# Gates and convolved inputs of layers 2 to 4 as z (1 + tanh(z/2)) in a four-layer hybrid decoder

## Chip, cores and metric

The kernel runs on one core of one Trainium2 chip. The metric is the device time of one execution in microseconds (us), the median over several runs. The core has a matrix engine (PE, with its weight loads shown as PEld), a vector engine (DVE), a scalar engine (ACT), GpSimd (POOL), and queues that move data between HBM and the on-chip memory SBUF; matmul results land in PSUM, from where ACT or DVE take them.

## What is computed

256 tokens of width 1024 pass four layers, each with another mixer (S5, gated linear attention, differential attention, Mamba-2 SSD), and each layer also attends to 256 memory tokens. Layers are counted 1 to 4 in the title and 0 to 3 in the code; below they have the code's numbers.

```python
for i in range(DEPTH):
    h = rms_norm(x, norm_g[i])
    # h @ W_in -> mixer inputs | z_mix | z_x | q_mem
    # every mixer ends in a gate by silu(z); layers 1 to 3 also normalise:
    #   gla:  rms_norm(o, norm_g) * silu(z)
    #   diff: rms_norm(o, subln_g) * (1 - lam_init) * silu(z)
    #   ssd:  xbc = silu(causal_depthwise_conv(xbc)); ... ; rms_norm(y * silu(z), norm_g)
    mem_out = memory_cross_attention(qx, mem_n, w_mem_kv[i], xq_g[i], xk_g[i]) * jax.nn.silu(z_x)
    x = x + jnp.concatenate([branch, mem_out], axis=-1) @ w_out[i]
```

silu(z) is z sigmoid(z), which equals z (1 + tanh(z/2)) / 2.

## The kernel before

All weights are streamed. SP's queue brings a raw tile of 128x1024 (L211); ACT rounds it to the matmul's number format (`hi`, L114, a cast), DVE takes the rest (`lo = raw - hi`, L115), and each product is made of three matmuls (`mm3`, L227 to L229: hi by hi, lo by hi, hi by lo). The right side is `hT`, the normalised activations, split in the same way, or `hT` is the weight side and the tile moves.

Projections are generators in a list, `fill`. A mixer's own code calls `tick` at chosen points, which lets the generator at the list's head issue a few more matmuls, so that PE has projection work between the mixer's small matmuls. Which instruction stands where on each engine's queue is settled by a scheduler ahead of time from the program, its priorities (scores are issued at a raised priority) and its estimates of durations; on the chip every engine then takes its own queue strictly in order and waits at an instruction whose inputs or buffers aren't ready.

PSUM is held in three small buffers (`ps`), one more (`ps2`) and two accumulators (`acc`) of two banks each. A matmul that starts a new accumulation waits until the reader of the old one is done.

The places that the change touches:

- `qx_zx_steps` (L456): the gate z_x of the memory attention, Silu by ACT from PSUM.
- Layer 1: `evac_z` (L940), the gate of a head, 128x1024, Silu by ACT from `acc`.
- Layer 2: `evac_z` (L1181), the same. `attend` computes scores (L1199) whose maximum DVE takes (L1200, L1202), exponentials on ACT (L1204), the difference of the two softmaxes on DVE (L1208 to L1210, tile `pr`), its transpose on PE (L1220), a copy on ACT (L1222, `wT`) and the product with v on PE (L1224). After the fourth head of a block comes the norm of the block: a copy and a square on ACT (L1231, L1232), sums on DVE (L1234 to L1236), the mean (L105), a power on POOL (L107, tile `rr`), one product (L1238), and four products with the gate (L1241), which PE then transposes (L188).
- Layer 3: `conv` (L1351 on ACT, three steps L1354 on DVE, Silu L1356 on ACT) for the tiles `bm`, `cm` and `xf`, and `evac_z` (L1369). `scan` makes decays: PE fills `ps` (L1400, L1401), ACT takes exponentials from it (L1404, L1405, tile `mt`), DVE multiplies them by dt and by `cb` (L1406, L1407), and PE uses `mt` in L1417. `cb` is a product of `cm` and `bm` that ACT copies out of PSUM (L1392).

Where a function of another kind than the last one runs on ACT, the program holds an instruction ACT_TABLE_LOAD ahead of it, under the line of that function.

Of the kernel before, what the change touches and what calls it, by code (L numbers as in the profile page):

```python
# [12 lines left out]
AF = mybir.ActivationFunctionType  # L13
# [24 lines left out]
class Net:  # L38
# [97 lines left out]
    def all_gains(self):  # L136
        a = self.a
        flat = lambda v: v.rearrange("a b -> (a b)")
        self.mem_g, self.s5_d, self.gla_b, self.ssd_g, self.gla_g, self.diff_g, xq, xk = self.gains("gains", [
            (a["mem_norm_g"], 8), (a["s5_d"][0], 16), (a["gla_b_gk2"][0], 4), (a["ssd_norm_g"][0], 16),  # L140
            (a["gla_norm_g"][0], 4), (a["diff_subln_g"][0], 1), (flat(a["xq_g"]), 4), (flat(a["xk_g"]), 4)], self.nc.sync)
        self.qsc = self.const.tile([P, 4], F32, name="qsc")
        self.nc.vector.scalar_tensor_tensor(self.qsc, xq, float(P) ** -0.5, xk, MUL, MUL)

# [226 lines left out]
    def xattn(self, i, qx, zx, perm=False):  # L371


        nc = self.nc
        kT, v = self.kv
        self.headnorm(qx)
        self.tick()
        qT = self.head_T(qx, self.t4(self.xp, "xt", 3).rearrange("p (h t) -> p h t", h=4), self.qsc[:, i:i + 1])
        zv = zx.rearrange("p (h q) -> p h q", h=4)

        def scores(t):
            rs = self.sm(4, "xrs")
            pr = (self.t4(self.xp, "xt", 3) if t else self.t4(self.xp, "pr")).rearrange("p (h m) -> p h m", h=4)
            sums = self.sm(4, "xsum")
            for hp in range(2):
                s = self.ps().rearrange("p (h m) -> p h m", h=2)
                for hh in range(2):
                    h = hp * 2 + hh
                    nc.tensor.matmul(s[:, hh, :], qT[:, h, t * P:(t + 1) * P], kT[:, h, :], start=True, stop=True)  # L389
                mx = self.sm(2, "xmx")  # L390
                nc.vector.tensor_reduce(mx, s, AX.X, ALU.max, negate=True)
                for hh in range(2):
                    h = hp * 2 + hh
                    nc.scalar.activation(pr[:, h, :], s[:, hh, :], AF.Exp, bias=mx[:, hh:hh + 1],
                                         accum_out=sums[:, h:h + 1])
            nc.vector.reciprocal(rs, sums)
            nc.vector.tensor_tensor(pr, pr, bc(rs, 2, 256), MUL)
            return pr

        self.tick()  # L400
        prs = [scores(0)]
        self.tick()
        prs.append(scores(1))
        pTs = [self.t4(self.xp, "pT"), self.t4(self.xp, "xt", 3)]
        mo = self.t4(self.xp, "xt", 3).rearrange("p (h q) -> p h q", h=4)
        hi = self.t4(self.bp, "xq", 2, F32R).rearrange("p (k t) -> p k t", k=4)
        for hp in range(2):
            pT = pTs[hp].rearrange("p (h m q) -> p h m q", h=2, m=2)
            for hh in range(2):
                tp = self.ps().rearrange("p (m q) -> p m q", m=2)  # L410
                for t in range(2):
                    for mh in range(2):
                        nc.tensor.transpose(tp[:, mh, t * P:(t + 1) * P], prs[t][:, hp * 2 + hh, mh * P:(mh + 1) * P],
                                            self.ident)
                (nc.scalar.copy if hh else nc.vector.tensor_copy)(pT[:, hh], tp)  # L415
            self.tick()
            pv = (self.ps2() if hp else self.ps()).rearrange("p (h q) -> p h q", h=2)
            for hh in range(2):
                h = hp * 2 + hh
                for mh in range(2):  # L420
                    nc.tensor.matmul(pv[:, hh, :], v[:, mh, h * P:(h + 1) * P], pT[:, hh, mh, :], start=mh == 0,  # L421
                                     stop=mh == 1)
            hs = slice(2 * hp, 2 * hp + 2)
            if hp == 0:
                lo = self.t4(self.xp, "pT", 1, F32R).rearrange("p (k t) -> p k t", k=4)
            nc.vector.tensor_tensor(mo[:, hs], pv, zv[:, hs], MUL)
            if perm:
                self.split(mo[:, hs].rearrange("p k (h s j) -> p (k h) s j", h=2, s=4),
                           *(u[:, hs].rearrange("p k (h j s) -> p (k h) s j", h=2, s=4) for u in (hi, lo)))
            else:  # L430
                self.split(mo[:, hs], hi[:, hs], lo[:, hs])
        self.tick()
        return [(hi[:, k, :], lo[:, k, :]) for k in range(4)]

    def silu_tanh(self, z, t):

        nc = self.nc
        nc.scalar.activation(t, z, AF.Tanh, scale=0.5)
        nc.vector.scalar_tensor_tensor(z, t, 1.0, z, ADD, MUL)

    def qx_zx(self, *args):
        out = []
# [4 lines left out]
    def qx_zx_steps(self, out, xT, w, col, silu=True):  # L447

        nc = self.nc

        def evac_z(nb, ps):
            if nb == 0:
                out.append(self.t4(self.bp, "xq", 2))
            z = out[1].rearrange("p (h t) -> p h t", h=4)[:, 2 * nb:2 * nb + 2, :]
            if silu:
                nc.scalar.activation(z, ps, AF.Silu)  # L456
            else:
                nc.scalar.copy(z, ps)

        def evac_q(_, acc, c):  # L460
            out.append(self.t4(self.bp, "xq", 2))
            nc.scalar.copy(out[-1].rearrange("p (t c) -> p t c", t=2), acc)  # L462

        return chain(self.linear_steps(xT, w, col + DX, DX, evac_q),
                     self.linear2_steps(xT, w, col, DX, evac_z, lambda: self.acc()[:, 0, :]))
# [279 lines left out]
    def layer0(self):  # L745
        nc, tc, a = self.nc, self.tc, self.a
        w = a["s5_w_in"][0]
        with self.pool("l0") as lp_:
# [52 lines left out]
            with self.pool("l0b") as p:  # L801
# [47 lines left out]

                self.norm_mem()  # L850
                self.mem_kv(0)
                self.silu_tanh(zx, self.t4(self.xp, "xt", 3))
                nc.vector.tensor_scalar(zx, zx, 0.5, None, MUL)
                self.fill = [self.linear2_steps(gp, a["s5_w_glu"][0], 0, DI, evac_glu)]
                moT = self.xattn(0, qx, zx, True)
                self.drain()
# [23 lines left out]
    def layer1(self):  # L880
# [4 lines left out]
        with self.pool("gla") as p:  # L885
# [51 lines left out]

            def evac_z(_, acc, c):
                vz.append(t4("z", 2))
                nc.scalar.activation(v2(vz[-1]), acc, AF.Silu)  # L940

            def proj(h):
                return chain(self.linear_steps(hT, w, 1024 + h * 512, 512, evac_v),
# [155 lines left out]
    def layer2(self):  # L1099
# [5 lines left out]
        with self.pool("diff") as p:  # L1105
# [11 lines left out]
            V.tensor_scalar(le[:, 3:4], le[:, 2:3], -lam_init, None, ADD)  # L1117
            nlam = le[:, 3:4]
            sg = p.tile([P, 4], F32, name="sg")
            V.tensor_scalar(sg, self.diff_g.to_broadcast([P, 4]), 1.0 - lam_init, None, MUL)  # L1120

            mask = p.tile([P, 256], F32, name="cmask")
            nc.gpsimd.memset(mask, 0.0)
# [49 lines left out]
            def proj(nb, out):  # L1173
                def evac_v(_, acc, c):
                    later.pop()()
                    out.append(t4("v", 2))
                    nc.scalar.copy(v2(out[-1]), acc)

                def evac_z(_, acc, c):
                    out.append(t4("z", 2))  # L1180
                    nc.scalar.activation(v2(out[-1]), acc, AF.Silu)  # L1181

                return chain(qk(nb, 0, *rt[0], out), qk(nb, 2048, *rt[1], out),
                             self.linear_steps(hT, w, 4096 + nb * 512, 512, evac_v),
                             self.linear_steps(hT, w, 6144 + nb * 512, 512, evac_z))
# [92 lines left out]
    def layer3(self):  # L1278
# [5 lines left out]
        with self.pool("ssd") as p:  # L1284
# [59 lines left out]
            def conv(col0, tag, bufs, out):  # L1344


                def evac(_, ps):
                    o = T([P, 2, 256], tag, bufs)
                    for c in range(2):
                        b = col0 // P + c  # L1350
                        nc.scalar.activation(o[:, c, :], ps[:, c, :], AF.Identity, bias=cw[:, 4, b:b + 1],  # L1351
                                             scale=cw[:, 3, b:b + 1])
                        for j in range(1, 4):
                            V.scalar_tensor_tensor(o[:, c, j:], ps[:, c, :256 - j], cw[:, 3 - j, b:b + 1], o[:, c, j:],  # L1354
                                                   MUL, ADD)
                    nc.scalar.activation(o, o, AF.Silu)  # L1356
                    out.append(o)

                return self.linear2_steps(hT, w, col0, 256, evac)
# [5 lines left out]
            def proj(gp, out):  # L1365
                def evac_z(nb, ps):
                    if nb == 0:
                        out.append(T([P, 4, 256], "z", 2))
                    nc.scalar.activation(out[-1][:, 2 * nb:2 * nb + 2, :], ps, AF.Silu)  # L1369

                return chain(conv(2048 + gp * 256, "bm", 2, out), conv(3072 + gp * 256, "cm", 2, out),
                             *(conv((2 * gp + i) * 256, "xf", 4, out) for i in range(2)),
# [2 lines left out]
            def scan(gp, bm, cm, xf0, xf1, zz):  # L1375
# [9 lines left out]
                def decays(b):  # L1385
                    gi, blk = b // 2, gp * 4 + b
                    if b % 2 == 0:
# [1 line left out]
                        nc.tensor.matmul(ps[:, 0:256], bm[:, gi, 0:P], cm[:, gi, :], start=True, stop=True)  # L1389
                        nc.tensor.matmul(ps[:, 256:384], bm[:, gi, P:], cm[:, gi, P:], start=True, stop=True)  # L1390
                        cbs.append(T([P, 384], "cb", 2))
                        nc.scalar.copy(cbs[gi], ps[:, :384])  # L1392
                    cb = cbs[gi]
                    ms = []
                    for j in range(2):
# [60 lines left out]
            def scale():  # L1456
                if not sc:
# [2 lines left out]
                        nc.tensor.matmul(ps[:, t:t + 1], ssa[:, t * P:(t + 1) * P], part32, start=True, stop=True)  # L1460
                    ss = self.sm(2, "ss2")
                    V.tensor_copy(ss, ps[:, :2])
                    sc.append(self.rstd(ss, 2, DI))
                return sc[0]

            cur, xs, pend, sc = [[] for _ in range(4)], [], [], []
# [82 lines left out]
```

## Time and profile before

| what | value |
|---|---|
| device time, median of 3 runs | 1427.86 us (1426.47 to 1428.77) |
| the profiled execution | 1432.01 us, its span 1430.3 us |
| mean granted clock of PE, share of full speed | 0.977 |
| PE busy | 1349.4 us, 94% of the span |
| DVE busy | 986.3 us, 1802 instructions |
| ACT busy | 809.7 us, 1331 instructions |
| POOL busy | 122.3 us |

Busy time is summed per engine. The profiled execution took 4.15 us longer than the median of the runs; rows read from its trace add up to its own span. Layer 0 lasts to about 495 us from the span's start, layer 1 to 760, layer 2 to 1128, layer 3 to the end.

### The profile page before, as it was taken

The page shows a single profiled execution, that of the slowest core. Times are in us where ns is not written, and L with a number is a line of the kernel's source. Part 1 is how long each engine was busy: PE and PEld are TensorE (multiplying, and loading weights), DVE is VectorE, ACT ScalarE, POOL GpSimd, SP SyncE. Part 2 cuts the span into 40 slices and gives each one's busy share as a digit, 9 for nine tenths or more (in the row PEclk, how much of TensorE's full clock was granted, in tenths as well). Part 3 has the DMA queues.
Part 4 walks back from the last instruction along what each step waited for, and adds up shares of the span by engine and source line. Part 5 has one row for each costly group of instructions (what it writes and reads, how often), then busy time and mean ns, then how long its engine had stood idle before and what let it go on. Part 6 is the DMA issues. An engine that isn't in the chain of part 4 may idle for free. (4 is left out here: it accounts for less than half of the span.)

```text
span 1430.3 us, 24119 instructions
## 1 busy us (share of the span) xinstructions
PE 1349.4 (94%) x9482; PEld 1099.7 (77%) x9482; DVE 986.3 (69%) x1802; ACT 809.7 (57%) x1331; POOL 122.3 (9%) x151
## 2 busy tenths in 40 slices
PE   5898887999999999999999999999999998899998
PEld 3575665889998787787787777787777897788976
DVE  6599999686555767664467587767765576666773
ACT  2573550565443568565455566577554467777762
POOL 1310000010002100000102021203002000000000
PEclk9999999999999999999999999999999899999999
DMA  5634122655655545554655445345345463455442
GB/s 166 124 93 134 50 60 82 201 148 161 177 190 179 168 118 167 155 148 133 175 185 169 139 123 172 123 143 156 110 132 153 120 177 103 119 145 143 125 148 74
DMA packets 175667, 199.86 MB, mean 140 GB/s; under 512 B 32330, under 2 KB 112451, under 8 KB 175555
## 3 DMA queue, kind: packets, MB, share of 16 engines
q1 hardware_dynamic: 173442, 193.72, 46.2%
q10 hardware_dynamic: 1280, 3.21, 0.8%
q0 software_dynamic: 832, 1.41, 0.6%
q8 instruction: 74, 1.21, 0.4%
q14 instruction: 39, 0.31, 0.1%
HBM read 194.64 MB, written 1.05 MB: 137 GB/s over the span
## 5 line engine op out<-in xcount | busy, mean ns | idle before, releaser
L115 DVE TENSOR_TENSOR lo<-raw,hi 128x1024 fp32r<-128x1024 f32 x331 | 400.5, 1214 | 242.2 <-ACT hi L114 238.8
L114 ACT CAST hi<-raw 128x1024 fp32r<-128x1024 f32 x331 | 343.6, 1040 | 352.1 <-PE acc L229 221.1
L227 PE MATMUL acc<-hi,hT 128*128 128x512 f32 (+1 forms) x576 | 234.0, 406 | 1.9 <-ACT v L936 1.2
L229 PE MATMUL acc<-hi,hT 128*128 128x512 f32 (+1 forms) x576 | 229.4, 399 | 1.5 <-DVE hT L118 1.3
L228 PE MATMUL acc<-lo,hT 128*128 128x512 f32 (+1 forms) x576 | 228.9, 397 | 0.0
L107 POOL TENSOR_TENSOR rr<-rv,mhalf 128x2 f32<-128x2 f32 (+3 forms) x34 | 71.7, 2108 | 1045.4 <-DVE rv L105 997.9
L227 PEld LDWEIGHTS acc<-hi,hT 128*128 128x128 f32 x576 | 111.3, 193 | 29.1 <-issue 3.4
L229 PEld LDWEIGHTS acc<-hi,hT 128*128 128x128 f32 x576 | 111.1, 193 | 27.6 <-DVE hT L118 2.8
L228 PEld LDWEIGHTS acc<-lo,hT 128*128 128x128 f32 x576 | 111.2, 193 | 22.6 <-issue 0.2
L227 PE MATMUL ps<-hT,hi 128*128 128x256 f32 (+1 forms) x328 | 97.5, 297 | 6.1 <-ACT mt L1405 4.3
L229 PE MATMUL ps<-hT,lo 128*128 128x256 f32 (+1 forms) x328 | 95.5, 291 | 0.6 <-DVE lo L115 0.6
L228 PE MATMUL ps<-hT,hi 128*128 128x256 f32 (+1 forms) x328 | 95.8, 292 | 0.0
L225 PE MATMUL acc<-raw,hT 128*128 128x512 f32 x160 | 79.3, 626 | 0.0
L227 PE MATMUL ps<-ghi,hi 128*128 128x256 f32 x256 | 72.3, 282 | 0.7 <-ACT xt L415 0.7
L229 PE MATMUL ps<-ghi,lo 128*128 128x256 f32 x256 | 71.7, 280 | 0.0
L228 PE MATMUL ps<-glo,hi 128*128 128x256 f32 x256 | 71.5, 279 | 0.0
L227 PEld LDWEIGHTS ps<-hT,hi 128*128 128x128 f32 (+1 forms) x328 | 64.0, 195 | 9.8 <-ACT mt L1405 4.9
L227 PE MATMUL acc<-hT,hi 128*128 128x256 f32 x224 | 65.0, 290 | 1.2 <-ACT xq L462 1.2
L229 PEld LDWEIGHTS ps<-hT,lo 128*128 128x128 f32 (+1 forms) x328 | 63.8, 195 | 1.4 <-DVE lo L115 0.8
L228 PEld LDWEIGHTS ps<-hT,hi 128*128 128x128 f32 (+1 forms) x328 | 64.1, 195 | 0.5
L229 PE MATMUL acc<-hT,lo 128*128 128x256 f32 x224 | 64.1, 286 | 0.0
L228 PE MATMUL acc<-hT,hi 128*128 128x256 f32 x224 | 63.5, 283 | 0.0
(483 smaller groups left out, 2855.6 us busy)
## 6 DMA issues: line engine op xcount, KB each, us to landing
raw<-in_w_out_dram SPq DMA_DIRECT2D x80, 512.0 KB, 3.7
raw<-in_diff_w_in_dram SPq DMA_DIRECT2D x72, 512.0 KB, 3.8
raw<-in_ssd_w_in_dram SPq DMA_DIRECT2D x56, 512.0 KB, 4.4
raw<-in_gla_w_in_dram SPq DMA_DIRECT2D x48, 512.0 KB, 4.0
raw<-in_s_w_in_dram SPq DMA_DIRECT2D x40, 512.0 KB, 4.7
raw<-in_w_mem_kv_dram SPq DMA_DIRECT2D x32, 512.0 KB, 3.7
raw<-in_s_w_glu_dram SPq DMA_DIRECT2D x32, 512.0 KB, 4.0
x<-in_x_dram ACTq DMA_DIRECT2D x1, 1024.0 KB
```

What stands on the lines that cost most here:

```text
L107: nc.gpsimd.tensor_tensor(r, v, self.mhalf[:, :n], ALU.pow)
L114: nc.scalar.copy(hi, src)
L115: nc.vector.tensor_tensor(lo, src, hi.bitcast(F32), SUB)
L225: mm(out, s[0], m[0], start=start, stop=stop)
L227: mm(out, s[0], m[0], start=start, stop=False)
L228: mm(out, s[0], m[1], start=False, stop=False)
L229: mm(out, s[1], m[0], start=False, stop=stop)
```

## The change

A new helper writes z (1 + tanh(z/2)), twice silu(z): ACT computes tanh into the output or into a scratch tile `t`, and one DVE instruction (scalar_tensor_tensor) forms (t + 1) z. It takes the place of every Silu in layers 1 to 3 and of an older helper in layer 0, where a DVE product by 0.5 falls away. The doubled values are set right in constants: the GLA norm's vector times 0.5, the SSD norm's vector times 0.25 and 16 times the count in its mean, 0.5 in the subln vector, 0.5 in the memory softmax (its product becomes a scalar_tensor_tensor), and 0.25 as a scale of the copy of `cb`.

Line numbers after L141 move by 3 and more: in the changed kernel the matmuls are L230 to L232, the helper's two instructions L442 (tanh) and L443 (product), scores L1202 to L1213, pr's transpose L1223, its product L1227, the block's norm L1234 to L1244, conv L1354 and L1357, `mt` L1407 to L1410.

```diff
+        for g, f in ((self.gla_g, 0.5), (self.ssd_g, 0.25)):
+            self.nc.vector.tensor_scalar(g, g, f, None, MUL)
...
-            nc.vector.tensor_tensor(pr, pr, bc(rs, 2, 256), MUL)
+            nc.vector.scalar_tensor_tensor(pr, pr, 0.5, bc(rs, 2, 256), MUL, MUL)
...
-    def silu_tanh(self, z, t):
+    def silu2(self, out, z, t=None):
         nc = self.nc
+        t = out if t is None else t
         nc.scalar.activation(t, z, AF.Tanh, scale=0.5)
-        nc.vector.scalar_tensor_tensor(z, t, 1.0, z, ADD, MUL)
+        nc.vector.scalar_tensor_tensor(out, t, 1.0, z, ADD, MUL)
...
-                nc.scalar.activation(z, ps, AF.Silu)
+                self.silu2(z, ps)
...
-                self.silu_tanh(zx, self.t4(self.xp, "xt", 3))
-                nc.vector.tensor_scalar(zx, zx, 0.5, None, MUL)
+                self.silu2(zx, zx, self.t4(self.xp, "xt", 3))
...
-                nc.scalar.activation(v2(vz[-1]), acc, AF.Silu)
+                self.silu2(v2(vz[-1]), acc)
...
-            V.tensor_scalar(sg, self.diff_g.to_broadcast([P, 4]), 1.0 - lam_init, None, MUL)
+            V.tensor_scalar(sg, self.diff_g.to_broadcast([P, 4]), 0.5 * (1.0 - lam_init), None, MUL)
...
-                    nc.scalar.activation(v2(out[-1]), acc, AF.Silu)
+                    self.silu2(v2(out[-1]), acc)
...
-                    nc.scalar.activation(o, o, AF.Silu)
+                    self.silu2(o, o, T([P, 2, 256], "jk", 2))
...
-                    nc.scalar.activation(out[-1][:, 2 * nb:2 * nb + 2, :], ps, AF.Silu)
+                    self.silu2(out[-1][:, 2 * nb:2 * nb + 2, :], ps)
...
-                        nc.scalar.copy(cbs[gi], ps[:, :384])
+                        nc.scalar.activation(cbs[gi], ps[:, :384], AF.Copy, scale=0.25)
...
-                sc.append(self.rstd(ss, 2, DI))
+                sc.append(self.rstd(ss, 2, 16 * DI))
```

The program held 47 ACT_TABLE_LOADs, and holds 10. It gains 8 products (t + 1) z of 128x1024 on DVE and 30 of 128x512. The scheduler also set some instructions in another order. Three places show what moved.

ACT in the scan of layer 3, ahead of the second pair of heads, before:

```order
L114 CAST hi_11520<-raw_11519 128x1024
L114 CAST hi_11526<-raw_11525 128x1024
L1351 ACTIVATE cm_11478<-ps_11429,cw_10733 128x256
L1404 ACT_TABLE_LOAD
L1404 ACTIVATE mt_11504<-ps_11501,ncum_11077 128x256
L1405 ACTIVATE mt_11504<-ps_11501,ncum_11077 128x128
```

The same place now:

```order
L114 CAST hi_11547<-raw_11546 128x1024
L114 CAST hi_11553<-raw_11552 128x1024
L1354 ACTIVATE cm_11503<-ps_11454,cw_10746 128x256
L1407 ACTIVATE mt_11531<-ps_11528,ncum_11096 128x256
L1408 ACTIVATE mt_11531<-ps_11528,ncum_11096 128x128
```

The table load between the convolution's first step and the exponential is gone; the rest stands as it did.

DVE at the start of the first scan of layer 3, before (the numbers behind the names are those of single buffers):

```order
L115 TENSOR_TENSOR lo_11425<-raw_11423,hi_11424 128x1024
L1354 SCALAR_TENSOR_TENSOR bm_11361<-ps_11312,cw_10733,bm_11361 128x255
L1354 SCALAR_TENSOR_TENSOR bm_11361<-ps_11312,cw_10733,bm_11361 128x254
L1354 SCALAR_TENSOR_TENSOR bm_11361<-ps_11312,cw_10733,bm_11361 128x253
L1406 SCALAR_TENSOR_TENSOR mt_11381<-mt_11381,dt_10767,cb_11374 128x256
```

And now:

```order
L115 TENSOR_TENSOR lo_11450<-raw_11448,hi_11449 128x1024
L1357 SCALAR_TENSOR_TENSOR bm_11384<-ps_11335,cw_10746,bm_11384 128x255
L1409 SCALAR_TENSOR_TENSOR mt_11406<-mt_11406,dt_10780,cb_11399 128x256
L1357 SCALAR_TENSOR_TENSOR bm_11384<-ps_11335,cw_10746,bm_11384 128x254
L1410 SCALAR_TENSOR_TENSOR mt_11406<-mt_11406,dt_10780,cb_11399 128x128
```

The first product of `mt` now follows one step of the convolution instead of three.

DVE in layer 2 where the attention of one projection block ends and that of the next begins, before: ss, rv, rr belong to the norm of the old block, dkap and pr to the scores of the new one, and z_7841 is the old block's gate:

```order
L1234 TENSOR_REDUCE ss_1327_8401<-sq_8398 128x4
L115 TENSOR_TENSOR lo_8523<-raw_8521,hi_8522 128x1024
L1208 RECIPROCAL dden_8480<-dden_8480 128x1
L1235 TENSOR_TENSOR ss_1327_8401<-ss_1327_8401,dsm_7844 128x4
L1209 SCALAR_TENSOR_TENSOR dkap_8491<-dden_8480,le,dsm_8414 128x1
L1236 TENSOR_TENSOR ss_1327_8401<-ss_1327_8401,dsm_7844 128x4
L1210 SCALAR_TENSOR_TENSOR pr_8481<-pr_8481,dkap_8491 128x128
L105 TENSOR_SCALAR rv_1328_8405<-ss_1327_8401 128x4
L115 TENSOR_TENSOR lo_8553<-raw_8551,hi_8552 128x1024
L1238 TENSOR_TENSOR rr_1329_8407<-rr_1329_8407,dsm_7844 128x4
L1241 SCALAR_TENSOR_TENSOR z_7841<-sq_8398,rr_1329_8407,z_7841 128x128 x2
```

And now (z_8396 is the next block's gate, the new product; pr_8427 is the new block's first):

```order
L443 SCALAR_TENSOR_TENSOR z_8396<-z_8396,acc_8316 128x1024
L1205 SCALAR_TENSOR_TENSOR dmx_8441<-dmx_8441,rq_7990 128x2
L1205 SCALAR_TENSOR_TENSOR dmx_8425<-dmx_8425,rq_7990 128x2
L1237 TENSOR_REDUCE ss_1327_8410<-sq_8407 128x4
L1238 TENSOR_TENSOR ss_1327_8410<-ss_1327_8410,dsm_7852 128x4
L1239 TENSOR_TENSOR ss_1327_8410<-ss_1327_8410,dsm_7852 128x4
L105 TENSOR_SCALAR rv_1328_8414<-ss_1327_8410 128x4
L1241 TENSOR_TENSOR rr_1329_8416<-rr_1329_8416,dsm_7852 128x4
L1211 RECIPROCAL dden_8426<-dden_8426 128x1
L1244 SCALAR_TENSOR_TENSOR z_7848<-sq_8407,rr_1329_8416,z_7848 128x128 x2
L1211 RECIPROCAL dden_8442<-dden_8442 128x1
```

Before, the new block's first two tiles `pr` were done on DVE ahead of the old block's norm, and splits of weights (L115) stood between its steps; now the norm stands in one row, and both tiles `pr` (L1213) follow it. PE, in turn, has the old block's last product (L1227) followed by 20 matmuls of a projection and then the transpose of pr_8427 (L1223); before, 18 projection matmuls stood ahead of that product (L1224) and 6 behind it. The same stands at the next block boundary.

## Rows read from the trace of the kernel before

**Rows 1.** The page's part 1: busy time, share of the span, instructions of each engine.

```profile
PE 1349.4 (94%) x9482; PEld 1099.7 (77%) x9482; DVE 986.3 (69%) x1802; ACT 809.7 (57%) x1331; POOL 122.3 (9%) x151
```

**Rows 2.** Waits of PE: who waited for whom, us in total, times, longest.

```profile
PE acc L1417 <- DVE mt L1406: 4.6, 2, 3.2
PE ps L227 <- ACT mt L1405: 4.3, 2, 2.1
...
PE ps L188 <- DVE z L1241: 0.7, 2, 0.4
...
PE ps L227 <- ACT pr L394: 0.5, 1, 0.5
...
PE acc L227 <- ACT z L940: 0.3, 1, 0.3
```

**Rows 3.** ACT's groups by line: busy us, mean ns | idle before.

```profile
L1404 ACT ACT_TABLE_LOAD x9 | 11.5, 1283 | 0.2
```

**Rows 4.** Timeline at 1197 us: start, duration, engine, line; idle before in brackets.

```profile
1197.59 1.28 ACT L1404 ACT_TABLE_LOAD   x1
...
1198.88 0.47 ACT L1404 ACTIVATE mt<-ps,ncum 128x256 f32<-128x256 f32 x1
...
1199.67 0.39 PE L227 MATMUL ps<-hT,hi 128*128 128x256 f32 x1 [2.14 <-ACT mt L1405]
```

**Rows 5.** Timeline at 1237 us, the same columns.

```profile
1236.93 1.22 DVE L115 TENSOR_TENSOR lo<-raw,hi 128x1024 fp32r<-128x1024 f32 x1 [0.19 <-ACT hi L114]
...
1238.08 0.99 DVE L1354 SCALAR_TENSOR_TENSOR bm<-ps,cw,bm 128x255 f32<-128x255 f32 x2
...
1239.19 0.49 DVE L1406 SCALAR_TENSOR_TENSOR mt<-mt,dt,cb 128x256 f32<-128x256 f32 x1
...
1239.73 0.65 PE L1417 MATMUL acc<-mt,xt 128*64 128x256 f32 x2 [3.21 <-DVE mt L1406]
```

**Rows 6.** Timeline from 1184 to 1187 us, the same columns.

```profile
1184.62 1.51 DVE L1354 SCALAR_TENSOR_TENSOR bm<-ps,cw,bm 128x255 f32<-128x255 f32 x3
...
1186.64 1.77 PE L1417 MATMUL acc<-mt,xt 128*64 128x256 f32 x6 [1.39 <-DVE mt L1406]
```

**Rows 7.** PE in stretches: us, busy (instructions), granted clock, DMA share, GB/s.

```profile
1186.60:1190.00 3.40, 3.36 (x12) 0.50 0.50 146
1200.20:1203.60 3.40, 3.40 (x18) 0.50 0.49 152
1241.20:1244.60 3.40, 3.40 (x14) 0.50 0.24 84
1253.20:1256.60 3.40, 3.40 (x28) 1.00 0.64 192
```

**Rows 8.** Timeline in layer 2, 877 to 885 us: the block's norm, ACT.

```profile
877.49 0.57 ACT L1231 COPY sq<-ps 128x512 f32<-128x512 f32 x1
...
878.90 0.63 ACT L1232 ACTIVATE sq<-sq 128x512 f32<-128x512 f32 x1
```

**Rows 9.** The same stretch, DVE.

```profile
880.64 0.68 DVE L1234 TENSOR_REDUCE ss<-sq 128x4 f32<-128x512 f32 x1
...
883.09 0.17 DVE L105 TENSOR_SCALAR rv<-ss 128x4 f32<-128x4 f32 x1
...
885.28 0.16 DVE L1238 TENSOR_TENSOR rr<-rr,dsm 128x4 f32<-128x4 f32 x1 [0.90 <-POOL rr L107]
885.48 0.61 DVE L1241 SCALAR_TENSOR_TENSOR z<-sq,rr,z 128x128 f32<-128x128 f32 x2
...
888.74 1.22 DVE L1153 TENSOR_TENSOR ro<-xq,rC 128x1024 f32<-128x1024 f32 x1
```

**Rows 10.** The same stretch, PE: two matmuls of a projection.

```profile
884.00 0.39 PE L228 MATMUL acc<-lo,hT 128*128 128x512 f32 x1
884.23 0.39 PE L229 MATMUL acc<-hi,hT 128*128 128x512 f32 x1
```

**Rows 11.** DVE's groups in layer 3 (1128 to 1430 us): busy, mean ns | idle before.

```profile
L115 DVE TENSOR_TENSOR lo<-raw,hi 128x1024 fp32r<-128x1024 f32 x75 | 91.7, 1223 | 62.0 <-ACT hi L114 59.6 <-PE ps L1401 2.4
```

## Prediction, made before the changed kernel ran

> **What bounds the kernel now.** I read the page's busy times first, then the waits of the matrix engine, then the timelines around its longest idle stretches. PE is busy for 94% of the span, DVE for 69% and ACT for 57% [rows 1]: PE sets the end, and what the change takes from ACT or gives to DVE counts only where PE stands still for it. A table load on ACT costs 1283 ns [rows 3]. The 47 in the program are 47 x 1.283 = 60.3 us of ACT, and 37 go, so ACT loses 47.5 us of work. Next to that the waits of PE that a load can have caused are small: 4.6 us for DVE's `mt`, 4.3 us for ACT's `mt` and 0.5 us for a softmax [rows 2]. Everything else lies beside matmuls. So at most 9.4 us of waiting can go, and the question is how much of it really hangs on the load, what it does to the clock, and what the new order puts in its place.
>
> **The change part by part, layer 3.** In each of two scans, at 1197 and at 1251 us (2.14 us each; two waits make the 4.3 us of [rows 2]), PE waits until ACT has emptied a `ps`. ACT goes from a convolution step into the load, 1.28 us, and the exponential starts at 1198.88, 0.01 us after the load's end; PE goes on at 1199.67 [rows 4]. The changed order has the same instructions without the load, and DVE isn't in this chain: -1.28 us each, -2.56 together, and 0.86 us of each wait stays.
>
> At 1237 us the wait is 3.21 us, and DVE's `mt` ends it [rows 5]. Without the load the exponential is done before 1238.08, but DVE is in a split until then (1236.93 + about 1.15), and does one convolution step of about 0.5 us (0.99 for two), also in the new order. `mt` then starts at 1238.58 in place of 1239.19: -0.6 us, not -1.28. What is late next is the weight split.
>
> At 1184 us the wait is 1.39 us. Before, three convolution steps (1.51 us from 1184.62) stand ahead of `mt` on DVE, and PE starts at 1186.64 [rows 6]. Now one stands there: `mt` can start at 1184.62 + 0.5 = 1185.12 and PE at 1185.12 + 0.54 (the distance from `mt` to PE in [rows 5]) = 1185.66. That is -1.0 us. A wait of 0.5 us for a softmax had a load in its chain and goes [rows 2]: -0.5. The waits of layer 3 lose 2.56 + 0.6 + 1.0 + 0.5 = 4.7 us.
>
> **The clock.** After the waits that ended at 1199.67 and 1239.73 PE ran 3.4 us at 0.50 of its granted clock, 1.2 in place of 2.4 GHz, and got through 18 and 14 matmuls, and the same after 1186.6; after the like wait that ended at 1253.2 it stayed at 1.00 and got through 28 [rows 7]. So 3.4 us at the lower level give about half the work; worked out from the matmul steps in such a stretch (0.21 against 0.12 us) it costs 1.5 us. Two of the three should go: those after 1186.6 and 1200.2, where 0.4 and 0.86 us of waiting are left. The third follows a wait of which 2.6 us stay. -3.1 us, with bounds 0 (all three stay) and -4.6 (all go).
>
> **Layer 2, an added wait.** Here the new order costs something. At two block boundaries the norm of the old block now stands on DVE in one row, and behind it in the queue are the two tiles `pr` that PE's next transpose needs, and behind these the weight splits. PE has 20 matmuls of 0.23 us (distance of the starts [rows 10]) to pass the time: 20 x 0.233 = 4.66 us. The norm takes: copy and square on ACT, 0.57 + 0.63 [rows 8]; sum 0.68; three instructions of the size of L105's 0.17, together 0.4; from L105's start to L1238, POOL's power between, 885.28 - 883.09 = 2.19; 0.20 to the first gate product; two pairs of gate products 1.22 [rows 9]; and two dkap and the first `pr`, taken as one such pair, 0.6. Sum 6.5 us. PE stands still for 6.5 - 4.66 = 1.8 us, and a little more because the copy only starts when the old product has left PE: I take 2.0 us per boundary, with bounds 1.0 (neighbours overlap by 0.1 us at each of the nine steps) and 2.5. The 0.7 us that PE now loses at these two places to the same norm [rows 2] goes, since the transposes of the gate now stand behind it: 2 x 2.0 - 0.7 = +3.3 us. A wait of 2 us may bring the lower clock with it, as one did at 1197 and one at 1251 didn't [rows 4, 7]: between 0 and two stretches of 1.5; I take one, +1.5.
>
> **The rest.** In layer 1 the gate was released by ACT alone; now DVE's product follows, 1.22 us for 128x1024, priced by a like instruction [rows 9]. PE waits there once, 0.3 us [rows 2]; I take +0.3, between -0.3 and +1.2. DVE gains 8 x 1.22 + 30 x about 0.7 (between 0.49 for 128x256 in [rows 5] and 1.22 for 128x1024) = 31 us in all. In layer 3 the weight splits have 62.0 us of idle time ahead of 75 instructions, 0.83 us each [rows 11]; a product of 0.7 us fits into that on average. Cover gone, each would cost up to 0.7 us: the rival below. The factors in the constants are free: two products of a few columns at the start, and instructions that only change their form. Layers 0 and 1 have other loads that go, all beside matmuls: nothing.
>
> **Sum.** -4.7 - 3.1 + 3.3 + 1.5 + 0.3 = -2.7 us on an execution of 1432.0. The profiled execution lies 4.15 us above the median of the runs; the difference is carried over to the median: 1427.86 - 2.7 = 1425.2 us. A measurement of this kernel can tell about 0.2%, 2.9 us, from no change, so this forecast lies just at that edge.
>
> **Rivals.** First, **full gain without the layer 2 wait**: the chain there is shorter than its sum by the overlap of its steps, or PE finds its matmuls long enough. For it: each step is short and handed on quickly. Against it: DVE works strictly in order, and the power on POOL alone takes half of PE's reserve. Then -4.7 - 3.1 = -7.8, 1420.1 us, and 1418.5 if the third clock stretch goes too.
>
> Second, **slower, by late weight splits in layer 3**: 24 new products of 0.7 us stand in DVE's queue among the splits, 16 of them in the convolutions, which also wait for ACT's tanh, so that the split behind them waits as well. It decides from the point where the lead of a split falls under 0.7 us; the mean is 0.83 [rows 11], so some must lie under it. If a third of the 24 cost PE their full length, that is 8 x 0.7 = +5.6 us; with both clock stretches in layer 2 (+1.5 more) the sum is -2.7 + 5.6 + 1.5 = +4.4, 1432.3 us. Against it: PE's waits for a split are not among the larger ones of the trace, and four weight tiles are kept.
>
> Third, **a switch costs more than its load**. In the rows the exponential follows the load by 0.01 us and the load follows the instruction ahead of it as closely [rows 4, 3]; a hidden cost would have to lie in the instructions around it. If it were as long as the load, the two waits of 2.14 us would go whole, -0.86 each, and the sum would be -4.4, 1423.5 us. The Trainium skill ("ScalarE: Activation LUTs", section What ACT_TABLE_LOAD costs) gives such a cost: about 1283 ns for the load and about 1380 ns of drain behind it, 2.66 us a switch. The trace here agrees with the first number and shows no drain.
>
> That the change doesn't take the loads away is no case, since 10 are left in its program.
>
> **How the numbers follow.** The forecast, 1425.2 us, has a chance of 0.55; its own range is 1422 to 1429, so about 0.22 of it lies below 1425.0 (faster by over 0.2%) and 0.33 within 0.2%. Full gain 0.20, all faster. The hidden cost of a switch 0.04, faster. Late splits 0.17, all slower. 0.04 is left for what I don't see, half of it within 0.2% and half slower. Faster 0.46, same 0.35, slower 0.19. The range reaches from the full gain with the third clock stretch, 1418.5, to 1431 us, which leaves out about 0.05 below and 0.13 above.
>
> **What would show each step right or wrong.** In layer 3 the waits of PE for ACT's `mt` should be about 0.9 us where they were 2.14, the wait at the second scan for DVE's `mt` about 2.6 us, and the one at the first under 0.5; the granted clock from 1150 to 1230 us should stay at full speed. In layer 2 PE should wait about 2 us, twice, for DVE's `pr` at the transpose L1223, and no longer for the gate. If these two waits are missing, the first rival holds; if PE's waits for `lo` grow, the second. Wrong would be most of all a new wait of PE at a place that I took for covered: in layer 1 for the gate, or in layer 3 for the convolved tiles, which now end on DVE.

## The result and the profile after

The changed kernel takes 1438.61 us (median of 4 runs, 1437.17 to 1439.17) beside 1427.36 us for the kernel before in the same series: a recorded ratio of 1.0072, 95% interval 1.0059 to 1.0086 (the two medians by themselves give 1.0079). It is 11 us slower. The forecast was 1425.2 us with a range up to 1431.0, so the time lies outside the range and on the other side. The profiled execution took 1439.17 us, its span 1436.7 us.

The table loads did go: the profile after has 10 of 1283 ns each where before had 47, and ACT is busy for 763 us where it was busy for 810 [rows 1]. The busy times, from the page's part 1:

```profile
PE 1348.3 (94%) x9482; PEld 1098.6 (76%) x9482; DVE 1010.6 (70%) x1841; ACT 763.2 (53%) x1294; POOL 118.5 (8%) x151
```

PE has the same work and the same busy share. What differs is where it waits. Waits of PE after, who waited for whom, us in total, times, longest:

```profile
PE ps L1440 <- ACT jk L1437: 6.7, 1, 6.7
...
PE acc L1025 <- ACT d L1029: 2.5, 2, 1.6
...
PE ps L1223 <- DVE pr L1213: 2.3, 2, 1.1
...
PE ps L1403 <- ACT sel L1401: 1.7, 1, 1.7
...
PE ps L230 <- ACT mt L1408: 0.9, 2, 0.7
PE acc L230 <- ACT hi L114: 0.9, 1, 0.9
...
PE acc L1420 <- DVE mt L1409: 0.3, 1, 0.3
```

Set against [rows 2], the waits for `mt` have all but gone (4.6 and 4.3 us before, 0.3 and 0.9 now): the gain was made. But the other five lines shown have none like them before, and the first alone is 6.7 us. Where the time went is seen best by the starts of the same instruction in both traces. The changed kernel comes to layer 3 1.0 us behind (the first transposes behind a wait for `hT`, L164, now L167, start at 1128.35 us before and at 1129.31 after). PE reaches the first product of `cm` and `bm` (L1389, now L1392) at 1182.3 us before and at 1188.0 after, so that 4.7 us go at the layer's start; the experiment with the squares in `xf` comes back to them. In the second scan the changed kernel leads by 4.1 us (the 49th product of L1417, now L1420, starts at 1259.65 us before and at 1255.55 after): a gain of 9.8 us within some 75 us. At the last products ahead of the third group's norm it still leads by 2.8 us (1317.32 before, 1314.49 after). It reaches the last L1417 (now L1420) at 1395.3 us before and 1401.8 after, behind by 6.4 us. The gain of the scans is there, and one place takes 9.2 us back.

That place is the norm of layer 3's third group. ACT after (start, duration, line; idle before in brackets):

```profile
1315.44 0.55 ACT L1354 ACTIVATE bm<-ps,cw 128x256 f32<-128x256 f32 x1
1318.69 0.56 ACT L1354 ACTIVATE bm<-ps,cw 128x256 f32<-128x256 f32 x1 [2.70 <-DVE bm L1357]
1320.90 0.63 ACT L442 ACTIVATE jk<-bm 128x512 f32<-128x512 f32 x1 [1.64 <-DVE bm L1357]
1321.43 0.61 ACT L1437 ACTIVATE jk<-z 128x512 f32<-128x512 f32 x1
1322.28 0.63 ACT L1437 ACTIVATE jk<-z 128x512 f32<-128x512 f32 x1 [0.24 <-DVE bm L443]
```

and PE in the same stretch:

```profile
1314.49 0.87 PE L1420 MATMUL acc<-mt,xt 128*64 128x256 f32 x8
1322.10 1.94 PE L1440 MATMUL ps<-jk,ones 128*32 128x256 f32 x8 [6.74 <-ACT jk L1437]
```

The tanh of the convolution writes a scratch tile `jk`, and so do the squares of the norm; both rotate through the same two buffers. The scheduler has set the squares behind the tanh of `bm`. The tanh can only start when DVE is through with six steps of the convolution, and the second square must wait until DVE's product has read the tanh out of its buffer (0.24 us, released by L443). So the buffer itself holds up little; what costs is the squares' place in ACT's queue. PE has all eight matmuls of the squares in its queue ahead of the next projection, and stands still for 6.74 us.

The clock in four stretches after, the columns those of [rows 7]:

```profile
1320.50:1327.30 6.80, 5.20 (x23) 0.50 0.03 11
1163.50:1166.90 3.40, 3.40 (x19) 0.50 0.07 11
1200.00:1203.40 3.40, 2.68 (x24) 1.00 0.51 143
1241.00:1244.40 3.40, 3.40 (x30) 1.00 0.39 131
```

Behind the wait of 6.74 us the granted clock is at 0.50 for 6.8 us, of which PE is busy for 5.20; at half speed that is about 2.6 us more, and wait and clock together make up about the 9.2 us. Another such stretch is new at 1163.5. The stretches that stood after the scans' waits [rows 7] are gone.

### The profile page after: what moved, and what is told of

The parts are those of the page before. It is cut to its first block, busy times and chain, and to the rows that moved or that the text cites. A ratio compares the mean times of both kernels' runs of the same rounds, so it can differ in the third digit from the quotient of the medians.

```text
span 1436.7 us, 24137 instructions
## 1 busy us (share of the span) xinstructions
PE 1348.3 (94%) x9482; PEld 1098.6 (76%) x9482; DVE 1010.6 (70%) x1841; ACT 763.2 (53%) x1294; POOL 118.5 (8%) x151
## 3 DMA queue, kind: packets, MB, share of 16 engines
q10 hardware_dynamic: 1280, 3.21, 0.7%
q0 software_dynamic: 832, 1.41, 0.6%
## 5 line engine op out<-in xcount | busy, mean ns | idle before, releaser
L115 DVE TENSOR_TENSOR lo<-raw,hi 128x1024 fp32r<-128x1024 f32 x331 | 400.5, 1214 | 238.2 <-ACT hi L114 237.7
L230 PE MATMUL acc<-hi,hT 128*128 128x512 f32 (+1 forms) x576 | 233.6, 406 | 1.9 <-ACT v L939 1.2
L232 PE MATMUL acc<-hi,hT 128*128 128x512 f32 (+1 forms) x576 | 228.5, 397 | 1.5 <-DVE hT L118 1.3
L230 PEld LDWEIGHTS acc<-hi,hT 128*128 128x128 f32 x576 | 110.8, 192 | 28.8 <-issue 3.4
L232 PEld LDWEIGHTS acc<-hi,hT 128*128 128x128 f32 x576 | 110.7, 192 | 27.6 <-DVE hT L118 2.7
L230 PE MATMUL ps<-hT,hi 128*128 128x256 f32 (+1 forms) x328 | 98.4, 300 | 3.5 <-ACT xt L358 1.2
L232 PE MATMUL ps<-hT,lo 128*128 128x256 f32 (+1 forms) x328 | 96.6, 295 | 0.7 <-DVE lo L115 0.7
L230 PE MATMUL ps<-ghi,hi 128*128 128x256 f32 x256 | 72.2, 282 | 0.7 <-ACT xt L418 0.7
L232 PE MATMUL ps<-ghi,lo 128*128 128x256 f32 x256 | 71.6, 280 | 0.0
L230 PEld LDWEIGHTS ps<-hT,hi 128*128 128x128 f32 (+1 forms) x328 | 65.1, 199 | 7.3 <-issue 3.0
L230 PE MATMUL acc<-hT,hi 128*128 128x256 f32 x224 | 65.3, 292 | 2.2 <-ACT xq L466 1.2
L232 PEld LDWEIGHTS ps<-hT,lo 128*128 128x128 f32 (+1 forms) x328 | 65.0, 198 | 1.5 <-DVE lo L115 0.9
L232 PE MATMUL acc<-hT,lo 128*128 128x256 f32 x224 | 63.8, 285 | 0.0
```

The source lines that it names most:

```text
L115: nc.vector.tensor_tensor(lo, src, hi.bitcast(F32), SUB)
L230: mm(out, s[0], m[0], start=start, stop=False)
L232: mm(out, s[1], m[0], start=False, stop=stop)
```

## Experiments

Ten kernels were run, in three lots, each beside the kernel before (medians of 1427.28 to 1428.49 us).

**Squares in xf.** The dead tile `xf` takes the squares, so that `jk` belongs to the convolution alone.

```diff
-                        sq = T([P, 2, 256], "jk", 2)
+                        sq = xf[h]
```

> The changed kernel, but the squares of the SSD norm are written into the dead tile xf instead of into jk, so that the convolution's tanh alone rotates through jk. Theory A (the two users of jk wait for each other): PE's wait of 6.74 us for the square at 1315 us goes, and with it the stretch of 6.8 us at the lower clock behind it (about 3.1 us): 1438.6 - 9.8, about 1429 us. Rival B (DVE and ACT are simply late there, whoever holds jk): the wait moves to the next consumer, 1436 to 1439 us.

Measured: 1425.40 us, ratio 0.9987 (0.9971 to 1.0004), 13 us less than the changed kernel. ACT and PE there (first ACT, then PE):

```profile
1298.94 0.63 ACT L1437 ACTIVATE xf<-z 128x512 f32<-128x512 f32 x1 [1.24 <-DVE z L1424]
...
1312.14 0.63 ACT L1437 ACTIVATE xf<-z 128x512 f32<-128x512 f32 x1 [1.74 <-DVE z L1424]
```

```profile
1309.65 0.63 PE L1440 MATMUL ps<-xf,ones 128*32 128x256 f32 x4
...
1313.12 0.62 PE L1440 MATMUL ps<-xf,ones 128*32 128x256 f32 x4
```

The first square is done 13 us before the second, each is set where its gate is ready, the matmuls come in two fours, and PE doesn't wait for them. Theory A holds. The gain is some 4 us more than the 9.2 us of that place, and in the two traces these 4 us lie ahead of it, at the start of layer 3. From the wait for `hT` (L167) to the transposes of `cum` (L1487) PE takes 46.1 us in the changed kernel (1129.31 to 1175.4), 41.7 us here (1130.12 to 1171.8) and took 41.3 us before (L164 to L1484). The stretch at the lower clock in which it starts, PE in the changed kernel and then here:

```profile
1129.30:1146.40 17.10, 17.09 (x81) 0.50 0.23 65
```

```profile
1132.80:1143.00 10.20, 10.20 (x49) 0.50 0.36 103
```

Whether these 4 us come with the edit or with the clock of the two executions isn't shown.

**One buffer of jk for each user.** The same memory, dealt out.

```diff
-                    self.silu2(o, o, T([P, 2, 256], "jk", 2))
+                    self.silu2(o, o, T([P, 2, 256], "ct", 1))
...
-                        sq = T([P, 2, 256], "jk", 2)
+                        sq = T([P, 2, 256], "jk", 1)
```

> The changed kernel, with the two buffers of jk dealt out: one for the convolution's tanh, one for the squares of the norm; the memory is the same. Theory A (the loss at 1315 us comes from the two users waiting for each other): as the run with the squares in xf, about 1426 us, or up to 2 us more, since two squares then share one buffer. Rival B (two buffers are too few for each user): 1436 us or more.

Measured: 1424.14 us, ratio 0.9982 (0.9961 to 1.0003), and no wait for the square in the trace. So it is the sharing, by way of the order that it forces on ACT's queue, and not the amount of memory or DVE's load, which are the same here.

**Layer 3 back to Silu.** Convolution and gate of layer 3 as before, with their constants; the rest of the change stays.

```diff
-                    self.silu2(o, o, T([P, 2, 256], "jk", 2))
+                    nc.scalar.activation(o, o, AF.Silu)
...
-                    self.silu2(out[-1][:, 2 * nb:2 * nb + 2, :], ps)
+                    nc.scalar.activation(out[-1][:, 2 * nb:2 * nb + 2, :], ps, AF.Silu)
```

> The changed kernel with Silu back in layer 3 (convolution and gate, with their constants); layers 1 and 2 and the memory gates keep the tanh form. Theory A (half of the loss comes from layer 1, from the block boundaries of layer 2 and from the clock there, half from layer 3): about 1432 us. Rival B (all of the loss is layer 3's): 1427 us or less.

Measured: 1434.57 us, ratio 1.0058 (1.0034 to 1.0081). What is left of the change, in layers 0 to 2 and in the memory gates, costs about 7 us by itself. In layer 3 (1130 to 1400 us) PE waits as it did before:

```profile
PE acc L1420 <- DVE mt L1409: 4.6, 2, 3.2
PE ps L230 <- ACT mt L1408: 4.5, 3, 2.1
```

**Layer 3 alone.** Silu in layers 1 and 2 and in the memory gates, the softmax as before; layer 3 as changed.

```diff
-                self.silu2(z, ps)
+                nc.scalar.activation(z, ps, AF.Silu)
...
-                self.silu2(v2(vz[-1]), acc)
+                nc.scalar.activation(v2(vz[-1]), acc, AF.Silu)
...
-                    self.silu2(v2(out[-1]), acc)
+                    nc.scalar.activation(v2(out[-1]), acc, AF.Silu)
```

> The kernel before with the change in layer 3 alone (convolution and gate, with their constants); layers 1 and 2, the memory gates and the softmax as before. Theory A: the scans gain about 10 us, the start of the layer loses 4 and the square's wait 10: about 1431 us. Rival B (layer 3 carries no loss; layers 1 and 2 do): about 1420 us.

Measured: 1429.82 us, ratio 1.0013 (0.9997 to 1.0028). The scans' gain and the loss at the squares nearly cancel within one layer.

**Layer 3 alone, squares in xf.** Both diffs together.

> As the run with the change in layer 3 alone, and the squares of the norm in xf instead of jk. Theory A: the scans' gain stays and the square's wait goes, about 1421 to 1423 us, faster than the kernel before. Rival B (the wait for jk stands for a shortage of DVE): like the run without it, 1431 us.

Measured: 1417.51 us, ratio 0.9929 (0.9903 to 0.9955), faster than both kernels. PE's waits in layer 3:

```profile
PE ps L1404 <- ACT sel L1402: 1.7, 1, 1.7
...
PE ps L230 <- ACT mt L1409: 0.9, 2, 0.7
...
PE acc L1421 <- DVE mt L1410: 0.3, 1, 0.3
```

**Loads back.** The kernel of the run above, and behind each convolution's tanh a Silu of one column that brings the table loads back and leaves DVE the same instructions.

```diff
-                    self.silu2(o, o, T([P, 2, 256], "jk", 2))
+                    t_ = T([P, 2, 256], "jk", 2)
+                    self.silu2(o, o, t_)
+                    nc.scalar.activation(T([P, 1], "tn", 2), t_[:, 0, 0:1], AF.Silu)
```

> Layer 3 alone in the tanh form with squares in xf (1417.5 us), and behind each convolution's tanh a Silu of one column into a tile that nobody reads, so that 18 table loads are back in layer 3 while DVE's work stays the same. Theory A (the scans' gain of about 10 us is that of the loads, their waits and the clock behind these waits): 1425 to 1428 us, with PE's waits for mt of 1.2 us and more back at the scans. Rival B (the gain comes from the new order on DVE, which sets mt behind one convolution step): 1418 to 1420 us.

Measured: 1430.62 us, ratio 1.0021 (1.0004 to 1.0038): 13 us more than without the loads. PE's waits in layer 3:

```profile
PE ps L230 <- ACT mt L1411: 4.4, 3, 2.1
PE acc L1423 <- DVE mt L1412: 4.4, 2, 3.0
```

The waits of [rows 2] are back at their old lengths, with stretches at the lower clock at 1197 and 1238 us. But the old order on DVE is back too. At the first scan one convolution step stood ahead of the first `mt` in the kernel without the loads, and now three do, as before the change. DVE there, without the loads and then with them:

```profile
1179.30 0.48 DVE L1358 SCALAR_TENSOR_TENSOR bm<-ps,cw,bm 128x255 f32<-128x255 f32 x1
```

```profile
1181.93 1.51 DVE L1358 SCALAR_TENSOR_TENSOR bm<-ps,cw,bm 128x255 f32<-128x255 f32 x3
```

So this run gives back loads and order together, and together they are worth more than the forecast said: about 10 us in the scans of the two traces and 13 us in the time. ACT's waits are the loads' own, since in their chain DVE has no part [rows 4]. How DVE's waits divide between loads and order isn't shown, and rival B stays open for them. The 16 Silus of one column are part of the price and can't be told from it.

**The gates one by one.** All three have layer 3 in the tanh form and the squares in `xf`; the base is 1417.51 us. First the memory gates and the softmax alone:

> The change in layer 3 and in the memory gates and softmax of all layers, Silu for the gates of layers 1 and 2, squares in xf. Base is the run with layer 3 alone and squares in xf, 1417.5 us. In this kernel's program the second half of GLA's output stands directly behind the first, as in the changed kernel. Theory A (layer 1's two waits of 0.84 and 1.63 us come with the memory gate, not with the GLA gate): +2 us, about 1420 us, with these two waits in layer 1. Rival B (they come from the GLA gate's product): 1417 to 1418 us.

Measured: 1420.41 us, ratio 0.9949 (0.9928 to 0.9971). Waits of PE between 590 and 690 us:

```profile
PE acc L1025 <- ACT d L1029: 0.8, 1, 0.8
```

The expectation put both waits of layer 1 to the memory gate; only one is its own. Of the 2.9 us in the time, this trace shows 1.1 us at that wait and 1.5 us at a stretch at the lower clock in layer 3, behind a wait for `sel` that the base has too. Then layer 1's gates as well:

> The change in layer 3, the memory gates and layer 1's gates; Silu in layer 2; squares in xf. Theory A (layer 1's gates themselves cost nothing, the memory gate does): as the run with the memory gates, about 1420 us. Rival B (DVE's product of 1.22 us releases the accumulator late): 2 us more.

Measured: 1421.10 us, ratio 0.9958 (0.9943 to 0.9974), and the second wait comes with GLA's gate:

```profile
PE acc L1025 <- ACT d L1029: 2.5, 2, 1.6
```

Rival B was right on the place; its price, 0.7 us here, can't be told from nothing. Then memory gates and layer 2's gates, Silu in layer 1:

> As the run before in this list, and the gates of layer 2 in the tanh form too; only layer 1's gates stay Silu. Theory A: the two waits for pr at layer 2's block boundaries (1.13 us each against 0.7 in all before), the wait at 1028 us and the clock behind it add 2 to 4 us: about 1423 us. Rival B (they are hidden): as the run before.

Measured: 1423.23 us, ratio 0.9976 (0.9957 to 0.9995), about 3 us over the run with the memory gates, with intervals that overlap. Waits of PE between 800 and 1126 us:

```profile
PE ps L1223 <- DVE pr L1213: 2.3, 2, 1.1
...
PE ps L1202 <- ACT xt L418: 0.7, 1, 0.7
```

Neither line stands in the traces of the two runs before.

**Four buffers for sel.** The base kernel, and the wait of 1.7 us that it still has.

```diff
-                        sel = T([P, P], "sel", 2, F32R)
+                        sel = T([P, P], "sel", 4, F32R)
```

> Layer 3 alone in the tanh form with squares in xf (1417.5 us), and sel with four buffers in place of two, for PE's wait of 1.7 us for sel at the second scan's start. Theory A (sel's buffers hold ACT's cast back): the wait goes, about 1416 us, or 1414.5 with a stretch of the clock. Rival B (the cast is queued behind the exponentials on ACT): 1417 to 1418 us.

Measured: 1413.49 us, ratio 0.9908 (0.9877 to 0.9939); the profiled execution took 1420.27 us, the other three 1412.99 to 1413.84. In layer 3 the wait for `sel` is gone, and 0.9 us is left for the exponential:

```profile
PE ps L1404 <- ACT mt L1409: 0.9, 1, 0.9
```

This is the fastest version that was run. Only part of its 4 us has a row: the wait is 1.7 us, and the intervals of the two runs overlap (0.9877 to 0.9939 and 0.9903 to 0.9955).

## Why the prediction was wrong

**The step that failed is the cover of the convolution's own tiles.** The part on "the rest" priced the new products by DVE's time and found room for them, and put the convolution's tiles in layer 3 at nothing; its last sentence named them as the place where a new wait would be most of all wrong. It looked at the products and not at the scratch tile that they read: `jk` was named in the diff, with two buffers, and the squares of the norm use the same two. No row of before showed a wait there, since with Silu in place the squares had `jk` to themselves. In the traces it cost 9.2 us, 6.74 of them PE's wait and the rest the clock behind it, and with another tile for the squares the time fell by 13 us. Of these, some 4 us belong to the start of layer 3, where the forecast had no term; whether sharing brings them stays open. With the squares elsewhere the changed kernel ends at 1425.40 us, the very time of the forecast, but that is luck: the other sums were off in both directions, as follows.

**The scans were sized too small.** Forecast: -4.7 us of waits and -3.1 us of clock, -7.8 us. Measured: 9.8 us between the two traces, and 13 us from the run with loads and order back. PE's waits in the scans after:

```profile
1191.27 0.65 PE L1420 MATMUL acc<-mt,xt 128*64 128x256 f32 x2 [0.28 <-DVE mt L1409]
1193.76 0.39 PE L230 MATMUL ps<-hT,hi 128*128 128x256 f32 x1 [0.19 <-ACT mt L1408]
1201.84 0.39 PE L230 MATMUL ps<-hT,hi 128*128 128x256 f32 x1 [0.72 <-ACT mt L1408]
```

The forecast left 0.4 us for the first and 0.86 for the others; the wait for DVE's `mt` at the second scan, 3.21 us [rows 5], was to shrink to 2.6 and became 1.7 us for `sel`. With shorter waits all three stretches at the lower clock went from this trace, not two.

**Layer 2 was sized too large at its two places, and a third was missed.** Forecast: 2.0 us each. The block's norm after, first DVE, then PE:

```profile
874.13 0.17 DVE L105 TENSOR_SCALAR rv<-ss 128x4 f32<-128x4 f32 x1
875.42 0.16 DVE L1241 TENSOR_TENSOR rr<-rr,dsm 128x4 f32<-128x4 f32 x1 [1.12 <-POOL rr L107]
...
877.00 0.60 DVE L1213 SCALAR_TENSOR_TENSOR pr<-pr,dkap 128x128 f32<-128x128 f32 x2
```

```profile
877.48 0.30 PE L1223 MATMUL ps<-ident,pr 128*128 128x128 f32 x1 [1.14 <-DVE pr L1213]
```

The wait is at the place and for the tile that were named, 1.14 us here and 1.13 at the next boundary. The term that was off is POOL's: from L105 to the next product it took 1.29 us, where [rows 9] gave 2.19. Those 2.19 us were read where a weight split ran on DVE beside POOL's power, and the new order, printed with the change, has no split there; the last section shows what that does. No stretch of the lower clock follows these two waits. But in the memory attention at 1028 us PE waits 0.7 us more, with a stretch at the lower clock at 1030.4, and at the start of layer 3 it waits 0.9 us for a `hi`. The run with layer 2's gates has both of these, and the two runs on `jk` have them too; the kernels with Silu in layer 2 have neither, though their convolutions are the same. So both come with layer 2's gates, by way of the order. Which rule of the scheduler carries them there stays open.

**Layer 1 was sized too small, by a mechanism that was not seen.** Forecast +0.3, at most +1.2 us. Measured 0.84 and 1.63 us of waiting in place of 0.3. The timeline of ACT, DVE and PE at the second place after:

```profile
674.89 1.02 ACT L442 ACTIVATE z<-acc 128x1024 f32<-128x1024 f32 x1
...
676.16 1.21 DVE L443 SCALAR_TENSOR_TENSOR z<-z,acc 128x1024 f32<-128x1024 f32 x1
676.52 0.61 ACT L1029 ACTIVATE d<-acc 128x512 f32<-128x512 f32 x1
...
677.27 1.12 PE L1025 MATMUL acc<-v,att 128*128 128x512 f32 x2 [1.63 <-ACT d L1029]
```

Before, a projection's matmuls stood between the two halves of GLA's output, and their accumulator was free once ACT had read the gate. Now DVE's product reads the accumulator last, the scheduler has moved the projection behind the second half, and the second half waits for ACT's square of the first, which stands in ACT's queue behind the gate's tanh and two instructions of a split (L117, 0.83 us in all). The price isn't DVE's 1.2 us, but the work that stood in between. The first wait, 0.84 us, comes with the memory gate, as its run shows.

**The rivals.** The slower one had the right side and the wrong mechanism: PE waits for `lo` 2.4 us in all after, 2.3 before, so weight splits were not late. The full gain was there in the scans, with the third clock stretch, as that rival had it, but something else paid for it. The hidden cost of a switch is small: from the convolution step to the exponential behind it ACT took 1.87 us with a load between (1236.81 to 1238.68 us before) and 0.46 us without one. ACT before, and then in the run with layer 3 alone and squares in `xf`:

```profile
1236.81 0.56 ACT L1351 ACTIVATE bm<-ps,cw 128x256 f32<-128x256 f32 x1
...
1238.68 0.47 ACT L1404 ACTIVATE mt<-ps,ncum 128x256 f32<-128x256 f32 x1
```

```profile
1225.83 0.56 ACT L1355 ACTIVATE bm<-ps,cw 128x256 f32<-128x256 f32 x1
...
1226.29 0.46 ACT L1408 ACTIVATE mt<-ps,ncum 128x256 f32<-128x256 f32 x1
```

The difference is 1.41 us: the load's 1.28, and 0.13 us because the exponential starts 0.10 us before the end of the step ahead of it where no load stands between, while 0.03 us pass idle around a load. That stands against the 2.66 us of the Trainium skill ("ScalarE: Activation LUTs", section What ACT_TABLE_LOAD costs); the measurement decides.

## What to carry to other kernels

When one operation becomes two on different engines, the tile between them is the change: look up who else rotates through its buffers, and put the two users' places in the queues side by side, since a shared scratch tile ties one engine's early work to another's late work. Ask for each accumulator who reads it last now, and what stood between its users. Here taking table loads away paid only where PE, which bounds the kernel, waited behind them, in layer 3's scans; the form that paid was the change in that layer alone, with a scratch tile that was dead anyway.

## What was not expected of the hardware

The clock falls or stays after the same waits. The runs with layer 3 alone, without and with the squares in `xf`, have the same code in layers 0 to 2 and the like waits near 495 us (1.57, about 1.0 to 1.4, and 1.32 us). PE in the same stretch, first without:

```profile
496.50:503.30 6.80, 5.77 (x27) 0.52 0.35 106
```

and with:

```profile
496.50:503.30 6.80, 3.92 (x30) 1.00 0.43 133
```

The first is at half clock and the second at full, and the two traces drift apart by 3.8 us there. Single executions of one kernel differ by this much and more: 1412.99 to 1420.27 us for the fastest version. In the second scan it is the same: a wait of 1.72 us for `sel` is followed by a stretch at 0.50 in the runs with the memory gates and with layer 1's gates (from 1231.7 and 1233.9 us), and by none in the run with layer 3 alone and the squares in `xf`. So a difference of a few us between two runs can be the clock's alone. The second surprise is POOL's power of 128x4: at the first block boundary of layer 2 the same instruction took 1.91 us before and 1.01 us after. It goes by what runs beside it on DVE. Before, a weight split did:

```profile
883.16 1.22 DVE L115 TENSOR_TENSOR lo<-raw,hi 128x1024 fp32r<-128x1024 f32 x1
883.33 1.91 POOL L107 TENSOR_TENSOR rr<-rv,mhalf 128x4 f32<-128x4 f32 x1 [23.59 <-DVE rv L105]
```

After, DVE stood idle until POOL was done:

```profile
874.38 1.01 POOL L107 TENSOR_TENSOR rr<-rv,mhalf 128x4 f32<-128x4 f32 x1 [16.75 <-DVE rv L105]
```

In these two traces each of the 16 powers of 128x4 took 1.91 or 1.92 us where a split ran on DVE beside it, and 1.01 us where nothing did.
